# A streaming-encoder layer on one core: blocks of 4, 6 and 6 k-tiles, and another start of the in-projection

## The chip, the core and the metric

The kernel runs on one core of a Trainium2 chip. What counts is the device time of one execution in microseconds (us), as the median of several runs. The engines are TensorE (PE, matmuls; PEld is its weight load), VectorE (DVE), ScalarE (ACT), GpSimd (POOL) and SyncE (SP, which issues most DMAs).

## The reference

One layer, fp32, 256 positions of width 2048 (D). Only the first part is touched:

```python
mod = jax.nn.silu(c) @ ada_w[layer] + ada_b[layer]          # c: one vector of 2048
shift1, scale1, gate1, shift2, scale2, gate2 = jnp.split(mod[:, None, :], N_MOD, axis=-1)
h = _rmsnorm(x, norm1_g[layer]) * (1 + scale1) + shift1
proj = h @ w_in[layer]
u_a, v_a, q, k, v_b, gates = jnp.split(proj, cut, axis=-1)
...  # gMLP branch, banded attention, two branch projections, sigmoid gates, output projection
x = x + gate1 * mixed
h = _rmsnorm(x, norm2_g[layer]) * (1 + scale2) + shift2
y = _hierarchical_moe(h, ...)                               # 32 experts, two per position
x = x + gate2 * y
return _rmsnorm(x, final_g)
```

## The kernel before

**Stages.** A prologue normalizes and turns x; the in-projection makes u, v, q, k and v_gate (five "homes" of 1024 columns); then come gates, attention and gMLP, branch projections, the output projection, the router, and 32 experts whose weights are streamed from memory until the end.

**The in-projection.** The contraction over D is cut into 16 k-tiles of 128, and those into BLOCKS, four of four tiles. Loops: block, home, k-tile. For each block and home run_steps loads one piece of w_in (four k-tiles by 1024 columns, 2 MiB) and makes a step of each k-tile. A step splits the weights into a rounded high part, cast by ACT (line 315), and the low part that remains, subtracted by DVE (line 316), into one of two split buffers of the tile W; then PE does twelve matmuls of 512 columns: high part of h by high part of w (289), low by high (290), high by low (291). Line 289 and 290 can run before the subtraction is done, 291 cannot. At the end of a home the sums are copied (first block, ACT) or added (later blocks, DVE, line 350) into the home.

**The modulation.** The factors shift1 and scale1 for a block's k-tiles must be there before the block. ada_block(k0, n) makes them: it loads pieces of ada_w through the ring of raw buffers r0 to r3 (2 MiB each, shared with w_in, on SP's queue), and DVE multiplies each row tile by silu(c) and adds it up (lines 202 and 204, 128x1024). PE turns the sums (214), DVE reduces them (217), ACT applies them to the transposed x (227) and rounds the result (230, tile dC), and DVE makes the low part (231, tile dD). ada_block is a generator: while block b runs, every call of next(with_ada) in run_steps performs one step of the one for block b+1. With the last block runs `ada`, which makes the other four modulation vectors (lines 425 and 427, products of 128x1024) at a pace of PACE[0] = 0.75 steps for a call and goes on in later stages.

**The order.** Each engine executes its instructions in a fixed order, set when the program is built. A long piece of DVE work in front of a subtraction thus delays it, whatever could run instead.

**The prologue.** c, norm1_g, two parts of ada_b and gmlp_b_s are loaded into the rows of one tile on ACT's queue, then the two halves of x. The tile is turned, silu(c) is made, x is squared (ACT), scaled (ACT, line 251), turned by PE and copied from PSUM (ACT, 261), and the gMLP weights are turned and copied (267).

Of the kernel before, what the change touches and what calls it, by code (L numbers as in the profile page):

```python
# [36 lines left out]
CW = 1024  # L37
Q = 4
JQ = D // (Q * P)
BLOCKS = (4, 4, 4, 4)  # L40
PACE = (0.75, 1.0, 1.0, 0.8, 0.7, 0.7, 0.7)
OUT_CUTS = ((0, 1024), (1024, 512), (1536, 512))

# [2 lines left out]
def hybrid_block(  # L46
# [32 lines left out]
    def T(shape, tag, dt=F32):  # L79
        uid[0] += 1  # L80
        return sb.tile(list(shape), dt, tag=tag, name=f"{tag}_{uid[0]}")

    class Ring:
# [4 lines left out]
        def next(self):  # L88
            self.i = (self.i + 1) % len(self.tags)
            return self.tags[self.i - 1]  # L90
# [45 lines left out]
            tick()  # L136


    ident = T([P, P], "ident")
    make_identity(nc, ident)  # L140
    ones = T([P, P], "ones")
# [3 lines left out]


    xt = [T([P, D], f"x{t}") for t in range(NT)]
    rows = T([P, P], "a2")
    nc.vector.memset(rows, 0.0)
    r0 = 0  # L150
    for src in (
        c[0].rearrange("(j p) -> j p", p=P),
        norm1_g[0].rearrange("(j p) -> j p", p=P),
        ada_b[0, 0:D].rearrange("(j p) -> j p", p=P),
        ada_b[0, D : 2 * D].rearrange("(j p) -> j p", p=P),
        gmlp_b_s[0],
    ):
        nc.scalar.dma_start(out=rows[r0 : r0 + src.shape[0], :], in_=src)
        r0 += src.shape[0]
    for t in range(NT):  # L160
        nc.scalar.dma_start(out=xt[t], in_=x[0, t * P : (t + 1) * P, :])
    ws = [T([P, 4, P], "a0"), T([P, 4, P], "a1")]
    for i in range(2):
        nc.gpsimd.dma_start(out=ws[i], in_=gmlp_w_s[0, 4 * i : 4 * i + 4].rearrange("g t s -> t g s"))
    cps = bk.ps()
# [4 lines left out]
    nc.scalar.activation(sc, cols[:, 0:ND], AF.Silu)  # L170
    g1c = cols[:, 16:32]
    b_shift = cols[:, 32:48]
    b_scale = cols[:, 48:64]
# [7 lines left out]
    hl = T([P, ND, S], "dD", F32R)  # L181
    accs = Ring(["f0", "f4"])

    def ada_block(k0, n):

        w = n * P
        acc = accs.sb([P, 2, w])
        nj = 16 // n
        for j0 in range(0, ND, nj):
            rw = raws.sb([P, nj, 2, w])  # L190
            for m in range(2):
                nc.sync.dma_start(
                    out=rw[:, :, m, :],
                    in_=ada_w[
                        0, j0 * P : (j0 + nj) * P, m * D + k0 * P : m * D + k0 * P + w
                    ].rearrange("(j p) n -> p j n", p=P),
                )
            yield
# [21 lines left out]
        nc.vector.tensor_add(sh1[:, ks], sums[:, 0, :], b_shift[:, ks])  # L220
        nc.vector.tensor_add(sg1[:, ks], sums[:, 1, :], b_scale[:, ks])
        nc.vector.scalar_tensor_tensor(
            out=sg1[:, ks], in0=sg1[:, ks], scalar=1.0, in1=g1c[:, ks], op0=ALU.add, op1=ALU.mult
        )
        yield
        for j in range(k0, k0 + n):
            nc.scalar.activation(
                hx[:, j, :], hx[:, j, :], AF.Identity, bias=sh1[:, j : j + 1], scale=sg1[:, j : j + 1]
            )
            nc.scalar.copy(hh[:, j, :], hx[:, j, :])  # L230
            nc.vector.tensor_sub(hl[:, j, :], hx[:, j, :], hh[:, j, :].bitcast(F32))
            if j % 2 == 1:
                yield


    def inv_rms(ss, name):
# [4 lines left out]
        nc.gpsimd.tensor_tensor(out=rs, in0=ve, in1=mhalf, op=ALU.pow)  # L241
        return rs

    first = ada_block(0, BLOCKS[0])
    ss1 = T([P, NT], "ss1")
    scr = T([P, D], "e2")
    for t in range(NT):
        nc.scalar.activation(scr, xt[t], AF.Square, accum_out=ss1[:, t : t + 1])
    rs1 = inv_rms(ss1, "n1")
    for t in range(NT):  # L250
        nc.scalar.activation(xt[t], xt[t], AF.Copy, scale=rs1[:, t : t + 1])
    for j in range(0, ND, 2):
        tp = bk.ps()
# [7 lines left out]
        nc.scalar.copy(hx[:, j : j + 2, :], tp.rearrange("p (a b) -> p a b", a=2))  # L261
    wsT = T([P, 8, P], "f3")
    for i in range(2):
        tp = bk.ps()
        for g in range(4):
            nc.tensor.transpose(tp[:, g * P : (g + 1) * P], ws[i][:, g, :], ident)
        nc.scalar.copy(wsT[:, 4 * i : 4 * i + 4, :], tp.rearrange("p (a b) -> p a b", a=4))
    nc.gpsimd.memset(wsT[CH:P, :, 0:CH], 0.0)
    for _ in first:
        pass  # L270


    def run_steps(lh, ll, w, k0, n, c0, evac, with_ada=None, cw=CW, after=None):

        nhf = cw // 512
        npc = 4096 // cw
        pt = []

        def prods(k, wh, wl, close):
# [1210 lines left out]
```

## Time and profile before

| | us |
|---|---|
| median of 3 runs (1697.71 to 1699.96) | 1699.67 |
| the profiled execution's own time | 1701.3 |
| its span | 1699.5 |
| PE busy | 1539.8 (91%) |
| DVE busy | 952.0 (56%) |
| ACT busy | 484.6 (29%) |
| DMA | 625.25 MB, mean 368 GB/s |

The shares of busy time are means over stages with different limits. The page's slices show DMA at nine tenths or more in the second half and lower in the first; PE is near full in both, but there its matmuls are longer (0.63 us against 0.40). So the stage has to be looked at for each question: the windows for who is full, the list of waits for what PE waits for, and the timeline for one place.

### The profile page before, as it was taken

How to read it: one execution, taken by the hardware profiler on the slowest of the kernel's cores; microseconds unless marked ns; L12 is line 12 of the kernel's file. 1: busy time of each engine (PE TensorE's matmuls, PEld its weight loads, DVE VectorE, ACT ScalarE, POOL GpSimd, SP SyncE). 2: the span in 40 equal slices, each digit the busy share in tenths (PEclk: the TensorE clock that was granted, in tenths of full speed). 3: DMA queues.
4: the chain of work that ended last, by engine and by line, in shares of the span. 5: the costliest groups of instructions: out<-in, count | busy, mean ns of one | idle time of the engine just before them, and what ended most of it. 6: DMA issues, size and time to landing. Idle time of an engine off the chain costs nothing.

```text
span 1699.5 us, 18309 instructions
## 1 busy us (share of the span) xinstructions
PE 1539.8 (91%) x6749; PEld 875.2 (51%) x6749; DVE 952.0 (56%) x1334; ACT 484.6 (29%) x793; POOL 126.5 (7%) x377
## 2 busy tenths in 40 slices
PE   2999999999999999799998989988899898998986
PEld 2777778777887776553332333433343332342433
DVE  5789999998778879743432333323333233332334
ACT  4554345675444345331111111101111011110112
POOL 1000000000000000011110100101010010100101
PEclk9999999999999999799999999999999999999998
DMA  9988987797987886879999999999999999999996
GB/s 358 347 315 329 350 341 299 286 339 284 357 315 294 336 300 232 341 313 419 416 417 418 415 418 416 418 417 416 418 416 417 418 416 418 415 418 418 416 415 223
DMA packets 139902, 625.25 MB, mean 368 GB/s; under 512 B 5656, under 2 KB 11920, under 8 KB 106400
## 3 DMA queue, kind: packets, MB, share of 16 engines
q1 hardware_dynamic: 137376, 614.49, 91.2%
q10 hardware_dynamic: 992, 5.28, 0.8%
q0 software_dynamic: 1440, 4.27, 0.8%
q8 instruction: 55, 0.90, 0.2%
q14 instruction: 39, 0.32, 0.1%
HBM read 621.91 MB, written 2.10 MB: 367 GB/s over the span
## 4 chain that ended last, share of the span: by engine, by line
PE 47%; DMA 45%; DVE 4%; issue 1%; ACT 1%; SPq 0%; POOL 0%; POOLq 0%; DVEq 0%; ACTq 0%
DMA r<-in_w_dram 24%; PE b L291 10%; PE b L289 10%; PE b L1209 10%; PE b L290 10%; DMA dC<-in_w_dram 10%; DMA E<-in_w_dram 9%; DMA r<-in_ada_w_dram 2%; PE b L1234 2%; DVE W L316 1%; PE b L1075 1%; DVE f L427 1%; DVE f L204 0%; ACT W L315 0%; PE b L589 0%
## 5 line engine op out<-in xcount | busy, mean ns | idle before, releaser
L1262 DVE TENSOR_TENSOR dB<-dB,b 128x512 f32<-128x512 f32 x248 | 153.6, 682 | 326.0 <-PE b L1260 326.0
L315 ACT CAST W<-r 128x1024 fp32r<-128x1024 f32 (+1 forms) x224 | 220.9, 988 | 328.1 <-PE b L290 294.0
L1209 PE MATMUL b<-r,e 128*64 128x512 f32 x1008 | 267.1, 632 | 47.5 <-DMA r<-in_w_dram 47.5
L316 DVE TENSOR_TENSOR W<-r,W 128x1024 fp32r<-128x1024 f32 (+1 forms) x224 | 255.9, 1147 | 61.8 <-ACT W L315 60.5
L289 PE MATMUL b<-W,dC 128*128 128x512 f32 x704 | 284.7, 405 | 5.5 <-ACT dC L230 3.7
L290 PE MATMUL b<-W,dD 128*128 128x512 f32 x704 | 280.1, 398 | 0.0
L291 PE MATMUL b<-W,dC 128*128 128x512 f32 x704 | 267.4, 399 | 2.1 <-DVE W L316 1.9
L1252 ACT CAST f<-f 64x512 fp32r<-64x512 f32 x124 | 76.4, 616 | 581.8 <-DVE dB L1262 419.8
L1209 PEld LDWEIGHTS b<-r,e 128*64 128x64 f32 x1008 | 87.9, 144 | 216.3 <-issue 142.2
L427 DVE SCALAR_TENSOR_TENSOR f<-r,sc,f 128x1024 f32<-128x1024 f32 x123 | 157.5, 1281 | 4.5 <-DMA r<-in_ada_w_dram 3.6
L289 PEld LDWEIGHTS b<-W,dC 128*128 128x128 f32 x704 | 132.9, 189 | 40.8 <-ACT dC L230 4.1
L291 PEld LDWEIGHTS b<-W,dC 128*128 128x128 f32 x704 | 131.7, 189 | 38.2 <-DVE W L316 7.1
L290 PEld LDWEIGHTS b<-W,dD 128*128 128x128 f32 x704 | 132.9, 189 | 30.4 <-issue 0.5
L1209 PE MATMUL b<-dC,e 128*64 128x512 f32 x272 | 129.8, 633 | 19.2 <-DMA dC<-in_w_dram 19.2
L1209 PE MATMUL b<-E,e 128*64 128x512 f32 x256 | 118.4, 617 | 19.1 <-DMA E<-in_w_dram 19.1
L1225 DVE TENSOR_TENSOR f2y<-f2y,b 128x256 f32<-128x256 f32 x31 | 13.1, 422 | 201.3 <-ACT f2y L1224 201.3
L1209 PE MATMUL b<-W,e 128*64 128x512 f32 x256 | 123.7, 635 | 0.0
L1209 PE MATMUL b<-dD,e 128*64 128x512 f32 x256 | 119.4, 616 | 1.3 <-DMA dD<-in_w_dram 1.2
L1234 PE MATMUL b<-r,f2y 128*64 128x512 f32 (+1 forms) x512 | 110.0, 582 | 2.3 <-DVE f2y L1225 2.3
L1253 DVE TENSOR_TENSOR f<-f,f 64x512 fp32r<-64x512 f32 x124 | 85.1, 686 | 26.7 <-ACT f L1252 23.8
L1314 POOL COPY e<-a 128x64 f32 x256 | 68.8, 270 | 192.6 <-PE b L1209 190.2
L1217 ACT COPY f2x<-b 128x512 f32<-128x512 f32 x32 | 18.7, 585 | 210.8 <-PE b L1209 202.9
(307 smaller groups left out, 1548.3 us busy)
## 6 DMA issues: line engine op xcount, KB each, us to landing
r<-in_w_dram SPq DMA_DIRECT2D x93, 2048.0 KB, 28.3
r<-in_w_in_dram SPq DMA_DIRECT2D x36, 2048.0 KB, 8.2
r<-in_ada_w_dram SPq DMA_DIRECT2D x32, 2048.0 KB, 8.7
W<-in_w_dram SPq DMA_DIRECT2D x24, 2048.0 KB, 28.1
dC<-in_w_dram SPq DMA_DIRECT2D x24, 2048.0 KB, 28.2
dD<-in_w_dram SPq DMA_DIRECT2D x24, 2048.0 KB, 28.3
E<-in_w_dram SPq DMA_DIRECT2D x24, 2048.0 KB, 7.6
r<-in_ada_w_dram SPq DMA_DIRECT2D x32, 1024.0 KB, 10.0
```

The costliest lines, as they stand in the source:

```text
L289: nc.tensor.matmul(o, a, wh[:, cs], start=(k == k0), stop=False)
L290: nc.tensor.matmul(o, b, wh[:, cs], start=False, stop=False)
L291: nc.tensor.matmul(o, a, wl[:, cs], start=False, stop=close)
L315: nc.scalar.copy(wh, src)
L316: nc.vector.tensor_sub(wl, src, wh.bitcast(F32))
L427: nc.vector.scalar_tensor_tensor(out=acc, in0=rw[:, jj, :], scalar=sc[:, j : j + 1], in1=acc, op0=ALU.mult, op1=ALU.add,)
L1209: nc.tensor.matmul(pab[a * CH : (a + 1) * CH, :], xe[:, 8 * half + j, :], w[:, j // JQ, j % JQ, :], start=(half == 0 and j == 0), stop=(ha ...
L1234: nc.tensor.matmul(po[a * CH : (a + 1) * CH, 0:cw], act[:, j, :], w[:, j, o : o + cw], start=(j == 0), stop=(j == 3),)
L1252: pin(nc.scalar.copy(oh[r, a, :], og[r, b, :]))
L1253: pin(nc.vector.tensor_sub(oh[o, a, :], og[r, b, :], oh[r, a, :].bitcast(F32)))
L1262: pin(nc.vector.tensor_add(xa[:, t, d0 : d0 + 512], xa[:, t, d0 : d0 + 512], pr))
L1314: nc.gpsimd.tensor_copy(xe[:, JQ * q + j, :], Xg[q][j][:, ds(o, CAP)])
```

## The change

BLOCKS becomes (4, 6, 6). w_in comes in pieces of three k-tiles for the six-tile blocks. The modulation of six tiles is made by two ada_block of three tiles (products of 128x768), and `hurried` spreads their steps over the block before, more than one step a call where there are more steps than calls (46 steps in 25 calls in block 0, 46 in 40 in block 1).

For the first block ada_first replaces ada_block: the shift sums are made by PE (64x512 matmuls with a broadcast of silu(c) as the weights), the scale sums by DVE (128x512 products), and one-column matmuls add over the partitions. x is scaled by DVE, and half of the copies of the turned x are DVE's. The high part of h comes from ACT directly, the low part takes two DVE operations. The gMLP weights are turned later, among the steps. x is loaded first on ACT's queue, the small vectors first on SP's, and one on POOL's.

```diff
-BLOCKS = (4, 4, 4, 4)
+BLOCKS = (4, 6, 6)
...
     for t in range(NT):
         nc.scalar.dma_start(out=xt[t], in_=x[0, t * P : (t + 1) * P, :])
+    r0 = 0
+    for src, queue in (
+        (c[0].rearrange("(j p) -> j p", p=P), nc.sync),
+        (norm1_g[0].rearrange("(j p) -> j p", p=P), nc.sync),
+        (ada_b[0, 0 : 2 * D].rearrange("(j p) -> j p", p=P), nc.sync),
+        (gmlp_b_s[0], nc.gpsimd),
+    ):
+        small = queue.dma_start(out=rows[r0 : r0 + src.shape[0], :], in_=src)
...
+    def ada_first(n):
+        w = n * P
+        scb = T([P, ND, CH], "f4")
+        nc.vector.tensor_copy(scb, sc.unsqueeze(2).to_broadcast([P, ND, CH]))
+        pick = T([P, 1], "pick")
+        nc.vector.tensor_add(pick, ident[:, 0:1], ident[:, CH : CH + 1])
+        pacc = bk.ps()
+        part = T([P, 2, w], "f0")
+        for j0, nj, rw in ada_pieces(0, n):
+            for jj in range(nj):
+                j = j0 + jj
+                i = j % 2
+                nc.tensor.matmul(
+                    pacc[i * CH : (i + 1) * CH, 0:w], scb[:, j, :], rw[:, jj, 0, :],
+                    start=(j < 2), stop=(j >= ND - 2),
+                )
+                if j == 0:
+                    nc.vector.tensor_scalar(part[:, 1, :], rw[:, jj, 1, :], sc[:, 0:1], None, op0=ALU.mult)
+                else:
+                    nc.vector.scalar_tensor_tensor(
+                        out=part[:, 1, :], in0=rw[:, jj, 1, :], scalar=sc[:, j : j + 1], in1=part[:, 1, :],
+                        op0=ALU.mult, op1=ALU.add,
+                    )
+            yield
+        nc.scalar.copy(part[:, 0, :], pacc[:, 0:w])
+        tp = sk.ps()
+        for m, what in enumerate((pick, ones[:, 0:1])):
+            for i in range(n):
+                nc.tensor.matmul(
+                    tp[:, m * n + i : m * n + i + 1], part[:, m, i * P : (i + 1) * P], what,
+                    start=True, stop=True,
+                )
+        modulation(slice(0, n), tp[:, 0 : 2 * n].rearrange("p (a b) -> p a b", a=2))
+        for j in range(n):
+            s, b = sg1[:, j : j + 1], sh1[:, j : j + 1]
+            nc.scalar.activation(hh[:, j, :], hx[:, j, :], AF.Identity, bias=b, scale=s)
+            full = scr[:, j * S : (j + 1) * S]
+            nc.vector.tensor_scalar(full, hx[:, j, :], s, b, op0=ALU.mult, op1=ALU.add)
+            nc.vector.tensor_sub(hl[:, j, :], full, hh[:, j, :].bitcast(F32))
+        yield
...
+    def ada_of(k0, n, calls):
+        parts = [n] if n <= 4 else [3, n - 3]
+        blocks, steps = [], 0
+        for m in parts:
+            blocks.append(ada_block(k0, m))
+            steps += (4 if m > 2 else 2) + ND + 1 + (m + 1) // 2
+            k0 += m
+        return hurried(itertools.chain(*blocks), max(1.0, steps / calls))
+
+    def hurried(g, rate):
+        due = 0.0
+        while True:
+            due += rate
+            while due >= 1.0:
+                due -= 1.0
+                if next(g, "end") == "end":
+                    return
+            yield
...
     for t in range(NT):
-        nc.scalar.activation(xt[t], xt[t], AF.Copy, scale=rs1[:, t : t + 1])
+        nc.vector.tensor_scalar(xt[t], xt[t], rs1[:, t : t + 1], None, op0=ALU.mult)
...
+        if j % 4 == 0:
+            nc.scalar.copy(hx[:, j : j + 2, :], tv)
+        else:
+            nc.vector.tensor_copy(hx[:, j : j + 2, :], tv)
...
         npc = 4096 // cw
+        npc = -(-n // -(-n // npc))
...
-        nxt = ada if lastb else ada_block(k0 + n, BLOCKS[b + 1])
+        nxt = ada if lastb else ada_of(k0 + n, BLOCKS[b + 1], len(homes) * (n + -(-n // 4)))
```

In the rows of order below, each line is an instruction of an engine with its line of the kernel, its operation, the tiles (out<-in, with buffer numbers; W is the split buffer, r a raw piece, f the running sum of products) and its shape; xN is a run of equal ones. The lines move with the change: 315 becomes 407, 316 408, 289 to 291 become 381 to 383, 204 becomes 264, 350 442, 425 and 427 become 517 and 519.

DVE in the first block, before: products (L204) for the next block between the subtractions (L316) of pieces r_53 and r_59.

```order
L316 TENSOR_TENSOR W_63<-r_53_291,W_63 128x1024
L204 SCALAR_TENSOR_TENSOR f_47_235<-r_54_293,sc_92,f_47_235 128x1024
L316 TENSOR_TENSOR W_63<-r_53_291,W_63 128x1024
L204 SCALAR_TENSOR_TENSOR f_47_235<-r_54_293,sc_92,f_47_235 128x1024
L316 TENSOR_TENSOR W_63<-r_53_291,W_63 128x1024
L204 SCALAR_TENSOR_TENSOR f_47_235<-r_54_293,sc_92,f_47_235 128x1024
L316 TENSOR_TENSOR W_63<-r_59_364,W_63 128x1024 x2
```

The same place after: the first home's four subtractions (piece r_45), and the first two of the second (r_55).

```order
L408 TENSOR_TENSOR W_63<-r_45_239,W_63 128x1024 x3
L262 TENSOR_SCALAR f_46_241<-r_47_242,sc_93 128x768
L264 SCALAR_TENSOR_TENSOR f_46_241<-r_47_242,sc_93,f_46_241 128x768
L408 TENSOR_TENSOR W_63<-r_45_239,W_63 128x1024
L264 SCALAR_TENSOR_TENSOR f_46_241<-r_47_242,sc_93,f_46_241 128x768 x2
L264 SCALAR_TENSOR_TENSOR f_46_241<-r_53_277,sc_93,f_46_241 128x768 x4
L408 TENSOR_TENSOR W_63<-r_55_316,W_63 128x1024 x2
```

Where one product stood between two subtractions, six of a smaller width now stand in a row ahead of the second home's first.

DVE at the start of the last block, before: the first home's subtractions (piece r_146), with L427 for the other modulation vectors and L350 for the sums of the block before.

```order
L316 TENSOR_TENSOR W_63<-r_146_1382,W_63 128x1024
L350 TENSOR_TENSOR x_43_230<-x_43_230,b_141_1334 128x512
L350 TENSOR_TENSOR x_43_230<-x_43_230,b_142_1335 128x512
L350 TENSOR_TENSOR x_43_230<-x_43_230,b_143_1336 128x512
L350 TENSOR_TENSOR x_43_230<-x_43_230,b_144_1337 128x512
L316 TENSOR_TENSOR W_63<-r_146_1382,W_63 128x1024 x2
L427 SCALAR_TENSOR_TENSOR f_148_1388<-r_147_1386,sc_92,f_148_1388 128x1024 x2
L316 TENSOR_TENSOR W_63<-r_146_1382,W_63 128x1024
```

The same place after: the third subtraction of piece r_135, then those of the next piece, r_143.

```order
L517 TENSOR_SCALAR f_137_1264<-r_136_1262,sc_93 128x1024
L408 TENSOR_TENSOR W_63<-r_135_1258,W_63 128x1024
L519 SCALAR_TENSOR_TENSOR f_137_1264<-r_136_1262,sc_93,f_137_1264 128x1024 x3
L519 SCALAR_TENSOR_TENSOR f_137_1264<-r_138_1265,sc_93,f_137_1264 128x1024 x4
L408 TENSOR_TENSOR W_63<-r_143_1317,W_63 128x1024 x2
```

Seven products now stand between the third subtraction and the fourth; there were two between the third and the fourth.

## Rows read from the trace of the kernel before

**Rows 1.** The page: the chain of waits, shares of the span by engine.

```profile
PE 47%; DMA 45%; DVE 4%; issue 1%; ACT 1%; SPq 0%; POOL 0%; POOLq 0%; DVEq 0%; ACTq 0%
```

**Rows 2.** Windows: us; busy of PE, PEld, DVE, ACT, POOL; PEclk, DMA share, GB/s.

```profile
45.00:75.00 30.00, 30.00 (x120) 24.04 (x121) 23.17 (x23) 15.33 (x22) 0.00 (x0) 0.92 0.92 344
...
780.00:1600.00 820.00, 737.99 (x3128) 288.30 (x3126) 276.13 (x468) 105.70 (x218) 80.10 (x270) 0.96 1.02 417
```

**Rows 3.** Windows of the in-projection, the same columns.

```profile
160.00:200.00 40.00, 39.99 (x172) 31.90 (x171) 39.37 (x44) 15.89 (x18) 0.00 (x0) 1.00 0.83 298
...
240.00:280.00 40.00, 39.24 (x171) 30.90 (x170) 38.55 (x44) 18.25 (x20) 0.58 (x1) 1.00 0.89 343
```

**Rows 4.** PE's waits in 40 to 330: us in total, times, longest.

```profile
PE b L289 <- ACT dC L230: 3.7, 1, 3.7
PE b L291 <- DVE W L316: 1.7, 3, 1.2
```

**Rows 5.** The chain of waits in 0 to 60: start, us, what.

```profile
18.31 14.51 DMA r<-in_ada_w_dram
...
36.90 1.30 DVE f L204
38.24 1.13 PE b L214 x4
...
43.52 1.09 ACT dB L227 x2
44.61 0.30 ACT dC L230
44.96 0.80 PE b L289
```

**Rows 6.** DVE's timeline, operations of other sizes: start, us, operation, shapes.

```profile
16.69 0.75 DVE L202 TENSOR_SCALAR f<-r,sc 128x1024 f32<-128x1024 f32 x1 [6.52 <-DMA r<-in_ada_w_dram]
...
715.47 0.75 DVE L1052 SCALAR_TENSOR_TENSOR f<-E,f2x 128x512 fp32r<-128x512 f32 x1
...
720.58 0.69 DVE L1067 COPY f2x<-b 128x512 f32<-128x512 f32 x1 [1.76 <-PE b L1063]
```

**Rows 7.** Timeline of ACT and DVE at 118 us: one step's cast and subtraction.

```profile
118.78 1.05 ACT L315 CAST W<-r 128x1024 fp32r<-128x1024 f32 x1 [1.75 <-PE b L290]
121.58 1.05 ACT L315 CAST W<-r 128x1024 fp32r<-128x1024 f32 x1 [1.75 <-PE b L290]
...
117.64 1.22 DVE L316 TENSOR_TENSOR W<-r,W 128x1024 fp32r<-128x1024 f32 x1
118.78 1.28 DVE L204 SCALAR_TENSOR_TENSOR f<-r,sc,f 128x1024 f32<-128x1024 f32 x1
```

**Rows 8.** DVE's timeline in the last block, a long stretch between two subtractions.

```profile
252.97 1.22 DVE L316 TENSOR_TENSOR W<-r,W 128x1024 fp32r<-128x1024 f32 x1 [0.28 <-ACT W L315]
254.11 2.60 DVE L427 SCALAR_TENSOR_TENSOR f<-r,sc,f 128x1024 f32<-128x1024 f32 x2
256.63 2.48 DVE L350 TENSOR_TENSOR E<-E,b 128x512 f32<-128x512 f32 x4
259.01 2.36 DVE L316 TENSOR_TENSOR W<-r,W 128x1024 fp32r<-128x1024 f32 x2
```

**Rows 9.** PE's timeline there.

```profile
260.29 1.20 PE L291 MATMUL b<-W,dC 128*128 128x512 f32 x4 [0.31 <-DVE W L316]
```

**Rows 10.** The chain at 670 us, and DVE's timeline in the router.

```profile
670.44 1.28 DVE f L427
...
717.55 1.27 DVE L427 SCALAR_TENSOR_TENSOR f<-r,sc,f 128x1024 f32<-128x1024 f32 x1
```

**Rows 11.** Groups of DVE's instructions in 40 to 330: count, busy, mean ns, idle before.

```profile
L316 DVE TENSOR_TENSOR W<-r,W 128x1024 fp32r<-128x1024 f32 x94 | 114.6, 1225 | 14.1 <-ACT W L315 13.6
```

**Rows 12.** Windows of the prologue's end, columns as in rows 2.

```profile
32.00:38.00 6.00, 0.00 (x0) 0.00 (x0) 5.73 (x5) 0.03 (x1) 0.07 (x1) 0.83 1.03 405
...
44.00:49.00 5.00, 4.04 (x10) 3.14 (x11) 4.03 (x7) 2.81 (x8) 0.00 (x0) 0.50 1.02 402
```

More of the change, by code (lines that the diff above doesn't have):

```diff
@@ L136, in flush @@
             tick()
+    rows = T([P, P], "a2")
+    nc.vector.memset(rows, 0.0)
     ident = T([P, P], "ident")
@@ L147, in hybrid_block @@
     xt = [T([P, D], f"x{t}") for t in range(NT)]
[L148 to L159, printed above, removed]
     for t in range(NT):
         nc.scalar.dma_start(out=xt[t], in_=x[0, t * P : (t + 1) * P, :])
+    r0 = 0
[6 more added lines that the diff above has]
+        small = queue.dma_start(out=rows[r0 : r0 + src.shape[0], :], in_=src)
+        if queue is nc.sync:
+            small_last = small
+        r0 += src.shape[0]
     ws = [T([P, 4, P], "a0"), T([P, 4, P], "a1")]
@@ L164, in hybrid_block @@
         nc.gpsimd.dma_start(out=ws[i], in_=gmlp_w_s[0, 4 * i : 4 * i + 4].rearrange("g t s -> t g s"))
+    nc.scalar.activation(mhalf[:, 1:2], mhalf[:, 0:1], AF.Silu)
+    nc.vector.memset(mhalf[:, 1:2], -0.5)
     cps = bk.ps()
@@ L169, in hybrid_block @@
     sc = T([P, ND], "sc")
-    nc.scalar.activation(sc, cols[:, 0:ND], AF.Silu)
+    sc_made = nc.scalar.activation(sc, cols[:, 0:ND], AF.Silu)
     g1c = cols[:, 16:32]
@@ L182, in hybrid_block, with ada_pieces @@
     accs = Ring(["f0", "f4"])
-    def ada_block(k0, n):
+    def ada_pieces(k0, n):
         w = n * P
-        acc = accs.sb([P, 2, w])
-        nj = 16 // n
+        nj = 4 if n > 2 or k0 == 0 else 8
         for j0 in range(0, ND, nj):
@@ L197, in ada_block, with modulation @@
                 )
+            yield j0, nj, rw
+    def modulation(ks, sums):
+        nc.vector.tensor_add(sh1[:, ks], sums[:, 0, :], b_shift[:, ks])
+        nc.vector.tensor_add(sg1[:, ks], sums[:, 1, :], b_scale[:, ks])
+        nc.vector.scalar_tensor_tensor(
+            out=sg1[:, ks], in0=sg1[:, ks], scalar=1.0, in1=g1c[:, ks], op0=ALU.add, op1=ALU.mult
+        )
[18 more added lines that the diff above has]
+                else:
+                    nc.vector.scalar_tensor_tensor(
+                        out=part[:, 1, :], in0=rw[:, jj, 1, :], scalar=sc[:, j : j + 1], in1=part[:, 1, :],
[9 more added lines that the diff above has]
+                    start=True, stop=True,
+                )
+        modulation(slice(0, n), tp[:, 0 : 2 * n].rearrange("p (a b) -> p a b", a=2))
[6 more added lines that the diff above has]
+        yield
@@ L198, in ada_block @@
+    def ada_block(k0, n):
+        w = n * P
+        acc = accs.sb([P, 2, w])
+        for j0, nj, rw in ada_pieces(k0, n):
             yield
@@ L219, in ada_block @@
             )
[L220 to L224, printed above, removed]
+        modulation(ks, sums)
         yield
@@ L242, in inv_rms @@
         return rs
-    first = ada_block(0, BLOCKS[0])
+    first = ada_first(BLOCKS[0])
+    with tc.issue_after(small_last.ins):
+        next(first)
     ss1 = T([P, NT], "ss1")
     scr = T([P, D], "e2")
-    for t in range(NT):
-        nc.scalar.activation(scr, xt[t], AF.Square, accum_out=ss1[:, t : t + 1])
+    with tc.issue_after(sc_made.ins):
+        for t in range(NT):
+            nc.scalar.activation(scr, xt[t], AF.Square, accum_out=ss1[:, t : t + 1])
     rs1 = inv_rms(ss1, "n1")
     for t in range(NT):
-        nc.scalar.activation(xt[t], xt[t], AF.Copy, scale=rs1[:, t : t + 1])
+        nc.vector.tensor_scalar(xt[t], xt[t], rs1[:, t : t + 1], None, op0=ALU.mult)
+    turned = Ring(["b2", "b3", "b4", "b5", "b6", "b0"])
     for j in range(0, ND, 2):
-        tp = bk.ps()
+        tp = turned.ps()
         for jj in range(2):
@@ L260, in hybrid_block, with turn_ws @@
                 )
-        nc.scalar.copy(hx[:, j : j + 2, :], tp.rearrange("p (a b) -> p a b", a=2))
-    wsT = T([P, 8, P], "f3")
[L263 to L270, printed above, removed]
+        tv = tp.rearrange("p (a b) -> p a b", a=2)
+        if j % 4 == 0:
+            nc.scalar.copy(hx[:, j : j + 2, :], tv)
+        else:
+            nc.vector.tensor_copy(hx[:, j : j + 2, :], tv)
+    with tc.issue_after(small_last.ins):
+        for _ in first:
+            pass
+    wsT = T([P, 8, P], "f3")
+    def turn_ws():
+        for i in range(2):
+            tp = sk.ps()
+            for g in range(4):
+                nc.tensor.transpose(tp[:, g * P : (g + 1) * P], ws[i][:, g, :], ident)
+            nc.scalar.copy(wsT[:, 4 * i : 4 * i + 4, :], tp.rearrange("p (a b) -> p a b", a=4))
+            yield
+        nc.gpsimd.memset(wsT[CH:P, :, 0:CH], 0.0)
+        yield
+    sides.append(turn_ws())
     def run_steps(lh, ll, w, k0, n, c0, evac, with_ada=None, cw=CW, after=None):
```

2 lines of the change are left out of this document (1 added, 1 removed).

## The prediction

> **What bounds the kernel now.** I read first the page's chain of waits: it is shared by TensorE (47%) and DMA (45%) [rows 1]. The windows say where each rules. From 780 us to the end the DMA engines are full at 417 GB/s [rows 2]: the experts' weights arrive as fast as they can, so that stage has a fixed length, and what the kernel loses or gains before it moves the end one for one. The in-projection ahead of it (45 to 282 us) is bound by PE, but only just: in 160 to 200 PE is busy 39.99 us of 40 and VectorE 39.37, in 240 to 280 39.24 and 38.55 [rows 3]. The list of PE's waits there names one large wait, 3.7 us before the first matmul, and 1.7 us behind W's low parts (L316) [rows 4]. So two things can be won: the start, and a microsecond or two of waits. And DVE has nothing to spare, so it matters in which order it gets its work.
>
> **The start.** The chain runs to the landing of the last adaLN piece (18.31 + 14.51 = 32.8), through four products on DVE, of which the last begins at 36.90 and ends at 38.2, then transposes, two reductions and two subtractions on DVE that stand between them, ACT at 43.52, and the first main matmul at 44.96 [rows 5]. The change leaves the bytes ahead of that last piece as they are (x, the vectors and four pieces), so it still lands near 32.9. What follows becomes shorter. DVE now does only the scale half: four products of 128x512 at 0.75 or less [rows 6] end at 32.9 + 4 x 0.7 = 35.7. Its new work, x's scaling (two of 128x2048, each two of the 128x1024 at 0.75: 3.0) and four copies from PSUM (4 x 0.69 = 2.8) [rows 6], lies in the time freed by the shift half, which went to PE: 20.4 us of products before (0.75 + 15 x 1.31) against 16 x 0.7 + 5.8 = 17. Behind the last product stand the column sums (1.0 with ACT's copy; an estimate from the 1.13 that four transposes took), three tiny DVE operations (0.5, an estimate) and four ACT operations (half of 1.09 each, 2.2); the reductions and subtractions no longer stand between. That is 39.4; then, by the order of ACT, a copy of the turned gMLP weights (0.55, as one of line 227) and the cast (1.05), 41.0, first matmul 41.2. With a handover of 0.1 to 0.2 us at each of eight steps I take 42.5, a gain of **2.5**; bounds 0.5 (DVE in arrears by 2 us) to 4.5 (everything as summed and the cast before the copy).
>
> **What DVE's new order costs.** This is the largest term. A step of the in-projection is a cast on ACT (1.05), the subtraction on DVE (1.22, next operation 1.14 later) and twelve matmuls in 2.80 us, the distance of the casts [rows 7]. There are two buffers: the cast of step k starts when the matmuls of k-2 have ended. Let h be the time of the matmuls that step k can do before its first L291 (L383 after), which needs the subtraction. It is needed at 2.80 + h after that start and done 1.05 + 1.22 after it, and the subtraction before it lay 2.80 earlier. So the distance between the starts of two subtractions may be 2.80 + 0.53 + h = 3.3 + h; what is longer, PE waits. The trace tests this: from 252.97 to 259.01 DVE did two products and four additions, 6.04; eight matmuls stood ahead (h = 8 x 0.233 = 1.9, free 5.2), so PE should lose 0.8, and it waited 0.31 [rows 8, 9]. The rule thus takes 0.5 too much, and I take 0.5 off each place below.
>
> In the old order one product stands between two subtractions. In the new one they stand in bunches. A product of 128x768 is priced at 1.03 (between 0.75 for 512 columns and 1.3 for 1024 [rows 6, 8]); the matmuls ahead are counted in PE's order of the changed kernel.
> - Block 0, its fifth step: six products, 1.14 + 6 x 1.03 = 7.3; two matmuls ahead, free 3.8; 3.5 - 0.5 = 3.0. The same bunch before the seventeenth: 3.0. Before the ninth four products, two reductions and an addition: 6.3 against 5.0, so 0.8. Sum 6.8.
> - Block 1: the longest is two reductions, additions and three products, at 5.9, with seven ahead (4.9): 0.5 after the deduction.
> - Block 2, fourth step: seven products of 1.28, 1.14 + 8.96 = 10.1; five ahead, 4.5; 5.6 - 0.5 = **5.1**. Later a stretch with four products and five operations of 0.6 (9.4 against 5.2) and soon another (7.8 against 5.2): 4.2 and 2.6, less 0.5 each, and since the first leaves the second half paid for (the wait moves all later casts too) I take 2.9 for both, with 5.8 as its upper bound.
> Together 15.3. Against it, the waits of before for L316 go (1.7 [rows 4]). Fewer blocks also take out twenty additions a quarter of a home each (60 to 40 of 0.62 = 12 us of DVE); that shortens DVE's work in blocks 1 and 2, but PE sets the time there, so it is worth only the waits already counted. In the last block the hurry adds eleven products, which are taken from the stages behind it.
> Bounds of this term: 0 (a bunch can only delay a subtraction, so no gain comes from it), if DVE's bunches meet PE at places where it waits anyway; 18 if the rule holds without the deduction, and 21 with both late stretches in full.
>
> **Behind the in-projection.** Eleven products leave the gates, the output projection and the router. At 670.44 one of them (1.28) stands in the chain, and four stand among the router's work (the first at 717.55) [rows 10], beside PE work that ends later. I take 1.5; 0 to 4.
>
> **DMA.** Block 0 now loads 10.5 MB of w_in and 12.6 MB of adaLN weights (half as much again as for four tiles), 23.1 MB where it was 18.9. At 344 GB/s with a share of 0.92 [rows 2], full engines would give 374, so 62 us; the block's twenty steps take 20 x 2.80 + 2 for the slow start = 58, with DVE's waits 65. So I count nothing, and if the waits don't come, 4 to 9 us of DMA take their place (rival B).
>
> **Sum.** The profiled run took 1701.3 (span 1699.5), 1.6 above the median. 1701.3 - 2.5 + 15.3 - 1.7 - 1.5 = 1710.9, less the 1.6: **1709**.
>
> **Rivals.**
> A, faster: the bunches cost nothing, because the pieces and casts come when DVE has run ahead, so that PE's two prepared steps and the time that it already loses at evacuations cover them. For it: DVE's subtractions wait 13.6 us for casts in 40 to 330 [rows 11], time in which it has nothing older to do; against: it runs in written order, and seven products of 1.28 are 9 us, longer than any two steps' spare. What is left is -2.5 - 1.7 - 1.5: 1699.7 - 5.7 = **1694**. It decides if the longest wait of PE for L408 stays under 1 us.
> B, the loads bind block 0: for it, 23.1 MB at the 344 GB/s that the trace shows are 67 us against 58; against, the engines were not full then. Taken without the bunches' waits in block 0, which it would hide: 1694 + 4 to 9, with the late bunches covered: **1698 to 1703**.
> C, the clock: the granted clock fell from 0.83 in 32 to 38, when PE did nothing, to 0.50 in 44 to 49 [rows 12], and ten matmuls at the start took 0.43 instead of 0.233: 2 us. In the changed kernel PE has matmuls of 64x512 until the last piece, then the column sums near 36. If they keep the clock up, 2 us go: **1707**. Against it, PE still does nothing for most of 36 to 42, about as long as before. (The Trainium skill, "TensorE: Matmul & The Clock Gate", Part 1 on the HAM clock gate, says that the clock is halved after idle time and comes back with activity; the trace agrees, with 0.50 after the idle stretch. By that rule C would hold only if the gap became short, and it would be 1707 instead of 1709.)
> D, the start doesn't come earlier: moving the vectors to the weights' queue and x to the front on ACT's only swaps who lands first. Then the gain of 2.5 is 0 to 0.5: **1711**. (The skill's "DMA: Bandwidth & Descriptors", in "Issuing engines are not separate DMA queues", says that transfers from all engines share the same 16 DMA engines. It speaks against a gain from queues; the landing at 32.8 is left where it was here for the reason of the bytes.)
>
> **Chances.** The forecast with its spread, 1703 to 1717: 0.46; D 0.08 and C 0.08 within the same range; A 0.24; B 0.14, about half of it inside 0.2%. A measurement of this kernel tells some 0.2% (3.4 us) from no change, so faster means under 1696.3 and slower over 1703.1. Faster 0.24, same 0.13, slower 0.63. The range takes in A and the upper bound of the bunches: 1709 + 8 = 1717, and 1694 below.
>
> **What would show it.** PE's waits for L408 over the in-projection: 12 to 16 us by the forecast, three of them over 2 us, in block 0 at its fifth and seventeenth step and at the fourth of block 2; under 3 us by A. Main matmuls should begin at 41 to 44, and the granted clock there should be 0.5 (forecast) or 1.0 (C). Waits of ACT's casts for w_in in block 0 speak for B. The MoE stage keeps its length to 1 us or so. I would be wrong if DVE's long bunches show no PE wait behind them, or if the late stages give back more than 4 us.

## The result, and the profile after

The changed kernel takes 1727.85 us (median of 5, 1726.56 to 1728.68), the kernel before 1699.96 beside it: a ratio of 1.016, 95% interval 1.0149 to 1.0172, 28 us slower. The direction was forecast, the size was not: 1709 was forecast, 1717 was the upper bound. The profiled execution has a span of 1726.0, 26.5 more than before.

The experts' stage, which was to pass on what comes before it, does so. A window of the changed kernel (us; busy of PE, PEld, DVE, ACT, POOL; PEclk, DMA share, GB/s) answers to [rows 2]:

```profile
780.00:1600.00 820.00, 741.71 (x3143) 288.29 (x3142) 274.62 (x465) 105.72 (x218) 82.59 (x272) 0.96 1.02 417
```

So the loss lies ahead of it. The last addition of the in-projection (line 350, now 442) starts at 305.8 where it started at 282.0: 23.8 of the 26.5 are there already. The start itself is earlier, as forecast: the chain of waits shows the first main matmul at 42.63, 2.3 us before that of [rows 5].

```profile
35.69 0.76 DVE f L231
36.49 1.88 PE b L240 x8
38.66 0.17 DVE sg L206
38.92 2.07 ACT dC L247 x4
40.99 0.48 ACT f L356
41.52 1.12 PE b L355 x4
42.63 0.62 PE b L381
```

The waits of PE in 30 to 360 (us in total, times, longest) answer to [rows 4]:

```profile
PE b L383 <- DVE W L408: 11.0, 6, 5.8
PE b L381 <- ACT W L407: 6.1, 6, 1.6
...
PE b L274 <- DVE f L264: 1.7, 3, 1.1
...
PE b L274 <- DVE sums L277: 0.7, 1, 0.7
```

The wait for the subtraction rose from 1.7 to 11.0, and a wait for the cast that was next to nothing is now 6.1. The longest is where it was forecast, at the last block's fourth step. DVE's timeline there, the seven products:

```profile
208.12 1.22 DVE L408 TENSOR_TENSOR W<-r,W 128x1024 fp32r<-128x1024 f32 x1
209.25 9.20 DVE L519 SCALAR_TENSOR_TENSOR f<-r,sc,f 128x1024 f32<-128x1024 f32 x7
218.37 2.35 DVE L408 TENSOR_TENSOR W<-r,W 128x1024 fp32r<-128x1024 f32 x2
```

and PE's:

```profile
213.43 0.39 PE L381 MATMUL b<-W,dC 128*128 128x512 f32 x1
219.64 1.22 PE L383 MATMUL b<-W,dC 128*128 128x512 f32 x2 [5.82 <-DVE W L408]
220.66 0.63 PE L382 MATMUL b<-W,dD 128*128 128x512 f32 x1
221.09 0.63 PE L383 MATMUL b<-W,dC 128*128 128x512 f32 x1
221.51 0.63 PE L381 MATMUL b<-W,dC 128*128 128x512 f32 x1
```

The second thing to see is behind the wait: the matmuls stand 0.43 us apart, not 0.233. The windows give the reason, the granted clock (column PEclk), which is 0.50 behind the wait, the lower of its two levels, and 1.00 again from 224 us:

```profile
220.00:223.00 3.00, 3.00 (x8) 2.33 (x8) 2.01 (x2) 0.39 (x1) 0.00 (x0) 0.50 1.02 408
224.00:228.00 4.00, 4.00 (x18) 3.19 (x17) 3.29 (x4) 1.05 (x1) 0.00 (x0) 1.00 1.02 374
```

So a wait of 5.82 cost 5.82 + nine matmuls at 0.195 more each = 7.6. The same stands behind the waits at 59.4 (nine matmuls) and 102.3 (some eleven), in block 0.

A balance from PE's timeline, from the first main matmul to the 960th (960 x 0.2333 = 224.0 in both): marked waits 20.1 (3.5 before), other work of PE 5.8 (4.2), and what is left over 11.9 (4.1). Of that, 51 matmuls at half clock make 9.9 (15 of them, 3.0, before). The three differences are 16.6, 1.7 and 7.8, less 2.5 for the start (42.46 on the timeline, 44.96 before): 23.6, against the 23.8 above.

A second place lies behind the in-projection, in the branch projections. DVE's timeline:

```profile
587.32 1.28 DVE L519 SCALAR_TENSOR_TENSOR f<-r,sc,f 128x1024 f32<-128x1024 f32 x1 [9.69 <-DMA r<-in_ada_w_dram]
588.52 2.35 DVE L408 TENSOR_TENSOR W<-r,W 128x1024 fp32r<-128x1024 f32 x2
```

and PE's:

```profile
589.80 2.07 PE L383 MATMUL b<-W,E 128*128 128x512 f32 x4 [6.98 <-DVE W L408]
591.67 0.63 PE L381 MATMUL b<-W,E 128*128 128x512 f32 x1
```

A product that waits for its piece stands ahead of two subtractions; PE waits 6.98 and goes on at half clock. In the kernel before this wait was 2.22:

```profile
565.05 0.80 PE L291 MATMUL b<-W,E 128*128 128x512 f32 x1 [2.22 <-DVE W L316]
```

### The profile page after: what moved, and what is told of

Same layout as the page of the kernel before. It is cut to its first block, busy times and chain, and to the rows that moved or that the text cites. A ratio compares the mean times of both kernels' runs of the same rounds, so it can differ in the third digit from the quotient of the medians.

```text
span 1726.0 us, 18414 instructions
## 1 busy us (share of the span) xinstructions
PE 1560.2 (90%) x6789; PEld 876.7 (51%) x6789; DVE 944.7 (55%) x1346; ACT 476.9 (28%) x784; POOL 127.5 (7%) x378
## 4 chain that ended last, share of the span: by engine, by line
PE 46%; DMA 43%; DVE 7%; issue 2%; ACT 2%; SPq 0%; POOL 0%; POOLq 0%; DVEq 0%; ACTq 0%
DMA r<-in_w_dram 21%; DMA dC<-in_w_dram 13%; PE b L1301 10%; PE b L383 10%; PE b L381 9%; PE b L382 9%; DMA E<-in_w_dram 7%; PE b L1326 2%; DVE W L408 2%; DMA r<-in_ada_w_dram 2%; DVE f L264 1%; DVE f L519 1%; PE b L1167 1%; ACT W L407 1%; DVE f L231 0%
## 5 line engine op out<-in xcount | busy, mean ns | idle before, releaser
L1301 PE MATMUL b<-r,e 128*64 128x512 f32 x1008 | 262.5, 627 | 46.9 <-DMA r<-in_w_dram 46.9
L381 PE MATMUL b<-W,dC 128*128 128x512 f32 x704 | 287.3, 408 | 7.2 <-ACT W L407 7.2
L383 PE MATMUL b<-W,dC 128*128 128x512 f32 x704 | 274.1, 402 | 12.0 <-DVE W L408 11.8
L1301 PEld LDWEIGHTS b<-dC,e 128*64 128x64 f32 x272 | 37.7, 144 | 82.2 <-issue 51.1
```

The costliest lines, as they stand in the source:

```text
L381: nc.tensor.matmul(o, a, wh[:, cs], start=(k == k0), stop=False)
L383: nc.tensor.matmul(o, a, wl[:, cs], start=False, stop=close)
L1301: nc.tensor.matmul(pab[a * CH : (a + 1) * CH, :], xe[:, 8 * half + j, :], w[:, j // JQ, j % JQ, :], start=(half == 0 and j == 0), stop=(ha ...
```

## Experiments on the bunches

**One part of the change at a time.** old_start is the kernel before with BLOCKS (4, 6, 6), pieces of three k-tiles and the paced modulation; start_only is the changed kernel with

```diff
-BLOCKS = (4, 6, 6)
+BLOCKS = (4, 4, 4, 4)
```

> The kernel before with blocks of 4, 6, 6 and the paced modulation alone: the old start, the old places of the small loads, x scaled by ACT. The bunches are the same (products of 128x768 in sixes before steps 8 and 16, seven products before step 53). If the blocks carry the loss, 1722 to 1728; if the new start carries a large part of it in its own right (the copies ahead of the casts on ACT), under 1718.

> The changed kernel with blocks of 4, 4, 4, 4: only the new start is left, and DVE's products stand one by one between the subtractions again. If the bunches of products (and the slow clock behind the waits they make) are the loss, all of it goes and the start's gain of 2.3 us (first main matmul at 42.63 where it was 44.96) is left: 1697.5 us. If the new prologue or the new places of the small loads cost something later, it stays over 1703.

old_start took 1724.99 (ratio 1.0152, 1.0136 to 1.0167), with the last addition at 305.6 and PE's wait of 5.8 at the same step: the blocks carry the loss, as expected. start_only took 1705.86 (1.0038, 1.0024 to 1.0052), not 1697.5: with blocks of four the kernel with the new start is 6 us slower than the one before, though it begins earlier. The second theory had the time (over 1703) but not the cause, the prologue or the small loads; start_evac below finds most of it elsewhere.

**Taking the bunches away.** no_lookahead loads the last units' adaLN pieces without one in advance, and the order has two products where it had seven. alternate_b0 gives DVE explicit order edges in block 0: a subtraction behind the last product written before it, a product behind the last subtraction.

```diff
# no_lookahead
-        ahead(1)
         start(0)
         for n, (i, q) in enumerate(pieces):
+            ahead(n + 1)
             rw = fetched[n]
-            ahead(n + 2)
...
# alternate_b0 (strict[0] is set in block 0 only)
-                    nc.vector.tensor_sub(wl, src, wh.bitcast(F32))
+                    with after_of(last_ada):
+                        last_sub[0] = nc.vector.tensor_sub(wl, src, wh.bitcast(F32))
                     if with_ada is not None:
-                        next(with_ada, None)
+                        with after_of(last_sub if strict[0] else [None]):
+                            next(with_ada, None)
...
```

> The changed kernel, but the adaLN pieces of the last block and of the later stages are loaded one at a time, not one ahead. In the order the seven products before the last block's fourth step become two, and the later bunches there go too. If the bunch is the cause, PE's waits in the last block (5.8, 0.4, 1.4 and 1.2 us) and the halved clock behind the long one (1.9 us) go: about 1718 us. If the loads are the cause, the products now wait longer for their piece and the time stays within 2 us of 1727.9 or rises.

> The changed kernel, but in the first block DVE has to keep the order in which products and subtractions are written, so no more than four products of 128x768 stand in a row. If the bunch is the cause, most of the waits of block 0 (1.6 + 1.6, 1.6 + 1.9 us) and the halved clock behind them (1.7 and 2.3 us) go: 1727.9 less 6 to 10, about 1719 us. If block 0 is bound by its loads (23.1 MB), it stays at 1726 or more, and ACT's casts wait for w_in.

> Both edits together: the blocks of 4, 6, 6 without the long bunches in block 0 and in the last block. If bunches are the loss and the two places add up: 1708 to 1710 us, still over the kernel before because of the 7 us wait in the branch projections at 590 us. If the waits only move to another place: over 1718.

They took 1718.38, 1717.68 and, both together, 1710.34 (ratios 1.011, 1.0104, 1.006, each within 0.002 either way). The first two are where the theory of the bunches had put them, the third 0.3 above its range. What each place cost, waits and clock together, shows on PE's timeline. With no_lookahead the 241st to the 960th main matmul (the last two blocks) take 175.9 us for 188.2; its last addition comes at 291.5, 14.3 earlier, but its span ends only 11.0 earlier, so some of the gain is lost behind it. With alternate_b0 block 0 (the first main matmul to the 240th) takes 66.3 for 73.4; of that 7.1, PE's waits give 3.6 (8.8 to 5.2) and the matmuls at half clock 3.5 (6.8 to 3.3). The slow matmuls cost there as much as the waits. DVE's timeline of no_lookahead at the last block's start shows the products spread (compare 209.25 above):

```profile
206.01 1.22 DVE L408 TENSOR_TENSOR W<-r,W 128x1024 fp32r<-128x1024 f32 x1
207.14 2.60 DVE L518 SCALAR_TENSOR_TENSOR f<-r,sc,f 128x1024 f32<-128x1024 f32 x2
209.66 1.22 DVE L408 TENSOR_TENSOR W<-r,W 128x1024 fp32r<-128x1024 f32 x1
210.79 1.27 DVE L518 SCALAR_TENSOR_TENSOR f<-r,sc,f 128x1024 f32<-128x1024 f32 x1
```

**The price of one bunch.** bunch_measured puts three, five and seven idle products (on a tile that nobody reads) ahead of three subtractions in block 0 of the kernel before.

```diff
+    BUNCH = {6: 3, 10: 5, 14: 7}
...
+                    n_extra = BUNCH.get(step_no[0], 0)
...
+                    for _ in range(n_extra):
+                        with tc.issue_after((last or prev_sub[0]).ins):
+                            last = nc.vector.scalar_tensor_tensor(
+                                out=dmy, in0=dmy, scalar=sc[:, 0:1], in1=dmy, op0=ALU.mult, op1=ALU.add
+                            )
...
```

> The kernel before, with 3, 5 and 7 products of 128x1024 on a tile that nothing else reads put in front of the subtractions of steps 6, 10 and 14 of the first block (0 is the first). With eight matmuls ahead (free distance 5.2) and the kernel's own operations, the distances are 7.5, 8.8 and 11.8 us: by the rule PE waits 2.3, 3.6 and 6.6, or 0.5 less each. If the clock is part of a bunch's price, the matmuls behind the longer waits take 0.43 us each for a while, and the run is 11 to 13 us plus 2 for each such wait over before: about 1714 to 1718. If only the wait counts: 1711 to 1713.

It took 1718.52 in its one run, 0.5 above the range of the theory with the clock and 5.5 above the one without. The three subtractions in question came 8.3, 8.7 and 11.2 us after the ones before (59.43 to 67.75, 75.47 to 84.17, 92.60 to 103.82 on DVE's timeline; the kernel's own products moved among them). With 5.2 free, the rule without a deduction gives 3.1, 3.5 and 6.0. PE's timeline:

```profile
69.02 1.21 PE L294 MATMUL b<-W,dC 128*128 128x512 f32 x4 [3.04 <-DVE W L332]
...
85.44 1.20 PE L294 MATMUL b<-W,dC 128*128 128x512 f32 x4 [3.40 <-DVE W L332]
...
105.10 2.07 PE L294 MATMUL b<-W,dC 128*128 128x512 f32 x4 [4.80 <-DVE W L332]
```

The third step also held a wait of 0.86 for a reduction, 5.7 in all. The rule 3.3 + h thus holds to 0.4 us, and the 0.5 that the prediction took off at each place was not due. The windows behind the three waits:

```profile
70.00:72.00 2.00, 2.00 (x6) 1.57 (x6) 2.00 (x3) 0.55 (x2) 0.00 (x0) 0.52 0.86 272
...
86.00:88.00 2.00, 2.00 (x10) 1.62 (x9) 2.00 (x3) 1.10 (x2) 0.00 (x0) 1.00 0.23 47
...
106.00:108.00 2.00, 2.00 (x6) 1.51 (x6) 0.99 (x3) 1.88 (x6) 0.00 (x0) 0.50 0.33 55
```

Half clock behind the first and the third, full clock behind the second, though its wait was longer than the first one's.

## Experiments on the rest

**ACT's order in block 0.** In start_only PE waited 5.3 us for casts at four ends of homes, and ACT's timeline has all four copies that empty a home ahead of the next casts:

```profile
53.44 2.68 ACT L440 COPY E<-b 128x512 f32<-128x512 f32 x4 [2.68 <-PE b L383]
56.01 2.00 ACT L407 CAST W<-r 128x1024 fp32r<-128x1024 f32 x2
```

The kernel before had a cast first:

```profile
55.54 1.05 ACT L315 CAST W<-r 128x1024 fp32r<-128x1024 f32 x1 [1.75 <-PE b L290]
56.49 1.97 ACT L348 COPY E<-b 128x512 f32<-128x512 f32 x3
```

start_evac and all_fixes force that:

```diff
-                    nc.scalar.copy(wh, src)
+                    last_cast[0] = nc.scalar.copy(wh, src)
...
             if begin:
-                nc.scalar.copy(o, p)
+                with tc.issue_after(last_cast[0].ins):
+                    nc.scalar.copy(o, p)
```

> Blocks of 4, 4, 4, 4 with the new start (1705.9 us), and ACT has to do the next home's first cast ahead of the four copies that empty a home in block 0, as the kernel before did. If that order is what the new start loses (PE waits of 1.6 us for a cast at four homes, 5.6 in all), they go and block 0 ends some 6 us earlier: 1699 to 1700, or up to 3 more, because a new bunch of small operations stands on DVE late in the last block. If the loss lies elsewhere (the loads, ACT's table), it stays at 1704 to 1706.

> Blocks of 4, 6, 6 with both edits against the bunches (1710.3 us) and the cast ahead of the copies in block 0. If the three orders are the loss and add up: 1704 to 1706, the 7 us wait in the branch projections still in it. If the larger first load stage (23.1 MB) binds block 0, the casts now wait for w_in instead and it stays over 1708.

start_evac took 1702.03 (1.0014, 1.0004 to 1.0023), within its range; its waits for casts up to 110 us fell from 5.3 to 0.3, and the last addition came at 279.4 where start_only had 288.2. That is 2.6 earlier than in the kernel before, and still the run is about 2 us slower; what is lost behind the in-projection there was not taken apart. all_fixes took 1711.79: with blocks of 4, 6, 6 the edit gives nothing, as its second theory had it. ACT's waits in 42 to 110 of that kernel (us in total, times, longest):

```profile
ACT W L416 <- PE b L390: 14.6, 7, 3.3
ACT W L416 <- DMA r<-in_w_in_dram: 12.3, 3, 6.0
```

The cast that now stands first waits for its piece of the weights, three times; in both_fixes, where the copies stand first, no cast waits for a load there. PE's 3.9 us for casts (both_fixes) turned into

```profile
PE b L391 <- DVE W L418: 2.6, 4, 1.0
PE b L277 <- DVE f L267: 2.2, 1, 2.2
```

**The late wait.** In the changed kernel the piece of 587.32 is asked for at 573.46 and the reload of x (2 MiB, on ACT's queue) at 573.67; the piece takes 13.8 us:

```profile
573.46 0.37 SPq L108 DMA_DIRECT2D r<-in_ada_w_dram  x1
573.67 0.39 ACTq L856 DMA_DIRECT2D dB<-in_x_dram  x1
```

Moving the reload in the program did not move it on the chip (issued at 573.99), so x_later says nothing on this; nor do its two companions, where it was issued at 550.86 (before: 550.45) and 550.47 (start_evac: 550.42). x_forced ties the reload to a later instruction of ACT, the output projection's first cast:

```diff
-        nc.scalar.dma_start(out=R.xa, in_=x[0].rearrange("(t p) d -> p t d", p=P))
...
+        with tc.issue_after(last_cast[0].ins):
+            nc.scalar.dma_start(out=R.xa, in_=x[0].rearrange("(t p) d -> p t d", p=P))
...
```

> The changed kernel, with the 2 MiB reload of x asked for one branch projection later; in its trace it is issued 0.2 us after an adaLN piece, whose products DVE then awaits for 9.7 us and PE for 7.0. If the reload shares the engines with that piece, the piece lands some 5 us earlier, PE's wait shrinks to about 2 and the halved clock behind it (1.9 us) goes: 1721 to 1723. If only the late place of the piece counts: 1727 to 1729.

> The kernel before with the reload of x one branch projection later: PE's wait of 2.2 us at 565 should go if the reload is what delays the piece: 1697 to 1698. If not: 1699 to 1700.

> Blocks of 4, 4, 4, 4, the new start with the cast ahead of the copies (1702.0), and the reload of x later: the 3.1 us wait at 566 should go, 1699 us; beyond noise better than the kernel before only if the later loads gain as well. If the reload isn't the cause: 1702.

> The changed kernel, with the 2 MiB reload of x held back until ACT has done the output projection's first cast, some 45 us later than in the run before it. If the reload shares the engines with the adaLN piece at 573 us, the piece lands in some 8 us where it took 13.8, DVE waits 4 us where it waited 9.7 and PE 2 where it waited 7.0, and the halved clock behind it may go: 1720 to 1723. If the piece is only asked for too late: 1726 to 1729.

> The kernel before, with the reload of x held back until ACT has done the output projection's first cast. Its adaLN piece at 550 us was issued 0.5 us ahead of the reload as well, and PE waited 2.2 us. If the reload delays it there too: 1697 to 1698. If the kernel before has slack at that place: 1699 to 1701.

x_later took 1726.12, before_x_later 1699.67, start_evac_x 1702.69: none moved the reload, and none changed its time by more than 2 us. x_forced, its reload at 607.40, took 1720.76 (1.0124, 1.0108 to 1.0139), 7 us less than the changed kernel: the reload is the cause of the late wait. Not all of the 7 is its doing: the last addition is 2.1 earlier there, ahead of the reload and with the same waits in block 0 (8.8 us in both), through an earlier start and fewer slow matmuls in that execution; behind the in-projection the gain is 5.8. SyncE's timeline has the piece asked for at 571.32,

```profile
571.32 0.37 SPq L108 DMA_DIRECT2D r<-in_ada_w_dram  x1
```

and on DVE's its products begin with no wait for it, 8 us later:

```profile
579.30 2.60 DVE L520 SCALAR_TENSOR_TENSOR f<-r,sc,f 128x1024 f32<-128x1024 f32 x2
```

PE's waits for subtractions in 520 to 660 are 0.9 there. The kernel before gains little from it: before_x_forced 1699.36 (0.9995, 0.9986 to 1.0004), no change that can be told; its piece was late too, but DVE had three products and two subtractions in hand (552.77 to 558.96).

**All together.**

```diff
# both_lookahead: the two edits against the bunches, but
-            ahead(n + 1)
+            ahead(n + 1 + (0 if in_proj[0] else 1))
# both_la_x_pace: also x_forced's edit, and
-PACE = (0.75,
+PACE = (0.47,
# all_fixes_pace: all_fixes with that pace; all_orders: both_la_x_pace with start_evac's edit
# start_la_x: start_evac with the look-ahead and x_forced's edit
```

> The same, and the last block's pace of adaLN steps is 0.47 for a call where it was 0.75, so that as many products are done there (19) as in the kernel before, and the later stages find the same rest of them. If the 7 us wait in the branch projections comes from the place that the products have reached, it shrinks to the 2.2 of before: 1697 to 1699. If it comes from the loads' order in any case, it stays: 1704 to 1706.

> The two edits against the bunches (1710.3), with the look-ahead of one adaLN piece back behind the in-projection. If the missing look-ahead is what the later stages lose (the part behind the in-projection was 3 to 5 us longer without it), 1705 to 1707; if not, 1709 to 1711.

> The same with the reload of x held back and 0.47 adaLN steps for a call in the last block (as many products there as in the kernel before). If the late losses are the look-ahead, the reload and the place that the products have reached, the later part is as long as in the kernel before and the in-projection ends within 3 us of it: 1698 to 1701. If the blocks of 6 lose in the later stages by themselves: over 1705.

> Blocks of 4, 4, 4, 4, the new start, the cast ahead of the copies, no look-ahead in the in-projection, the reload of x held back. If the three orders were all that stood against the new start, its 2.3 us are left and the 2 to 3 us wait at 565 goes as well: 1695 to 1698, faster than both kernels. If the late loads take it back: 1699 to 1702.

> Blocks of 4, 6, 6 with the edits against the bunches, the look-ahead behind the in-projection, the reload held back, the pace of 0.47 and the cast ahead of the copies in block 0. The last edit gave 3.5 us with blocks of 4 and nothing with blocks of 4, 6, 6, where DVE is then late in block 0. If it adds up with the rest: 1696; if block 0 has no room on DVE: 1698 to 1700, as without it.

all_fixes_pace took 1712.67, a time that neither of its theories had, though the late wait stayed, as the second said: its last addition came at 281.6, as early as in the kernel before, and then 11 us were lost behind it, 8.0 of them in one wait for a subtraction at 566. So the place that the products have reached does not by itself decide the late wait. both_lookahead took 1710.76, no better than both_fixes, with a late wait of 7.16 still there (at 573), so the look-ahead is not what the later stages miss. both_la_x_pace took 1699.26 (0.9995, 0.9986 to 1.0004): 28 us regained, and its span ends 29 us before that of the changed kernel, with the same blocks and the same start. PE's waits of it in the in-projection:

```profile
PE b L390 <- ACT W L417: 3.8, 3, 1.9
PE b L278 <- DVE f L268: 2.8, 3, 1.5
```

start_la_x took 1699.08 (0.9993, 0.9984 to 1.0002) and all_orders 1700.50 (1.0004, 0.9995 to 1.0013). None is faster than the kernel before by more than the measurement tells. Of the last 11.5 us between both_lookahead and both_la_x_pace, 3.7 are the pace's, in the last two blocks: the 241st to the 960th main matmul take 175.3 and 171.6 us there, and the pace alone makes the same difference between all_fixes and all_fixes_pace (175.3 and 171.6). The rest lies mostly behind the in-projection, where pace and reload were not separated; the reload alone gave 5.8 there in x_forced. Why the in-projection of start_la_x, which ends 4.7 us earlier (277.3 for 282.0), shows in the time with about 1 us is open.

## Why the prediction was wrong

**What bounds it, and that DVE's order decides:** right. The three places of the long bunches are the three where PE waits most.

**The start:** right in size, 2.3 for 2.5, but not by the terms of the sum. The last product ended at 36.45 and not at 35.7 (each took 0.78 for 0.7, and DVE came to the last four 0.3 after their landing); the column sums took 1.9 for 1.0; and four transposes of the gMLP weights, not a cast, stood last. The 1.3 us allowed for handovers covered the difference. The landing is as before (33.0 for 32.8) and the start came earlier, so D fell. C fell too: PE's longest idle stretch ahead of the main matmuls shrank from 7.6 to 2.5 us, and yet the granted clock was 0.50 in 42 to 46.

**The bunches' waits:** right in size, if a little low, and in part by luck. By place, forecast and measured: fifth step 3.0 and 3.2 (1.62 and 1.55), ninth 0.8 and 1.7, seventeenth 3.0 and 3.5, block 1 0.5 and 1.0, fourth step of the last block 5.1 and 5.8, the two later ones 2.9 and 2.9. Sum 15.3 and 18.1. The gap is the deduction of 0.5, taken from one wait of 0.31 [rows 9]; measured by itself the rule needs none. The luck is in block 0: at the fifth and the seventeenth step 1.62 of each wait is for a cast, not for the bunch's subtraction, and with the bunch out it stays (1.92 and 1.62 in alternate_b0). The rule gives the whole wait at such a place; the bunch by itself adds only 1.3 and 1.9 there.

**The size of the miss.** Without the 1.6 that was taken off at the end, the sum forecast 9.6 us for the profiled execution, and it was 26.5. Of the 16.9 between them, 3.0 are in PE's waits (16.6 more than before, where 15.3 less 1.7 was forecast), 7.8 in what is left over in the balance and 1.7 in other work of PE (both at nothing in the sum), and 4.2 behind the in-projection; 0.2 has no place.

**What failed first: a wait was priced at its length.** Behind the three long bunches PE's clock was granted at half, and the next nine to eleven matmuls cost 0.195 each on top. The rows to see it were there: after the idle stretch the same kernel ran at 0.50 [rows 12]. The prediction used them for the start alone and not for the waits that it forecast itself. Behind the waits of the bunches that is 6 of the 7.8 us left over in the balance. (The Trainium skill, "TensorE: Matmul & The Clock Gate", Part 1 on the HAM clock gate, says that the array's clock is halved after idling. The windows behind the wait of 5.82 and behind two of the three waits of bunch_measured agree, at 0.50 to 0.52; the third does not, at 1.00.)

**What failed second: "behind the in-projection", a gain of 1.5.** It became a loss of 2.7, through one wait of 6.98 where there had been 2.22, and the half clock behind it. That place cost some 6 us more than before; the rest of these stages gave back about 3, so a gain was there, and this place outweighed it. The prediction counted what the products do for DVE when there are fewer of them, not that the rest of them now meets the reload of x at another place. (The Trainium skill, "DMA: Bandwidth & Descriptors", "Issuing engines are not separate DMA queues", says that DMAs started by different engines run on the same 16 DMA engines and interleave. The trace agrees: beside a transfer on ACT's queue one on SyncE's queue took 13.8 us, and 8 at most without it in x_forced.)

**What failed third: an engine was left out.** ACT's order was read for the first cast only. That the copies of a home now stand ahead of the casts costs 5.3 us of waits in start_only. In the changed kernel this part is hidden in the bunches' waits (the 1.62 at the fifth and the seventeenth step), and with the bunches out and the cast put first (all_fixes) the casts wait 12.3 us for the weights instead.

**The rivals:** A fell with waits of 5.8 and 7.0; it would have needed none over 1 us. B, that the loads set block 0's length, was no explanation of the changed kernel's loss: no cast waits for weights there between 42 and 120. With the bunches out, block 0 still takes 65.4 to 66.4 us in alternate_b0, both_fixes and both_la_x_pace, where it took 59.6 before and 73.4 in the changed kernel. That is near B's estimate of 67, but it is no sign of B: start_only, with the smaller loads of four tiles, takes 66.1 as well. The windows, of both_la_x_pace and then of start_only, show PE about equally busy in the same 66 us; in start_only DVE is 11 us less busy and the DMA engines are at 0.88 for 0.95:

```profile
42.00:108.00 66.00, 60.65 (x255) 47.02 (x255) 58.55 (x66) 33.31 (x47) 0.70 (x1) 0.97 0.95 343
42.00:108.00 66.00, 60.16 (x249) 46.83 (x249) 47.80 (x47) 34.15 (x48) 0.52 (x1) 0.97 0.88 324
```

What the four runs have in common is the order of ACT: PE waits 3.8 to 5.3 us for casts behind the copies. Only where the cast is put first does something else appear: block 0 takes 67.7 in all_fixes, whose casts wait for the loads, and 61.1 in start_evac, with the same order of ACT and blocks of four. Whether the loads or DVE's larger work make those 6.6 us was not separated.

## What to carry to other kernels

Where two engines are both nearly full and one feeds the other, compare the order of work, not its amount: the distance between two feeding operations against what the buffers cover, place by place, on every engine in the chain. Price a long wait of TensorE at its length and, where the granted clock has fallen behind such waits, the slow matmuls too. And a change that shifts the pace of background work moves every later meeting of that work with other loads; go through the later stages for pieces that are asked for beside a large transfer.

## What was not expected of the hardware

The clock's fall does not follow the length of the wait alone: behind 3.04 us it was granted at 0.52, behind 3.40 at 1.00, behind 4.80 at 0.50, all in one run, and in the kernel before seven matmuls behind a wait of 2.22 (at 565) were slow too. And blocks of 6 k-tiles with a third fewer additions (40 for 60) brought no time at all once their orders were mended (1699.26 against 1701.11 in those runs): PE's own matmuls take 224 us of the in-projection's 238 (42.6 to 280.9) in that kernel. Its start is 2.5 earlier and its last two blocks 4.3 shorter (171.6 for 175.9), but block 0 is 5.8 longer than before and takes nearly all of that back.
